# Output gates and z as seven quarter products in a stage of their own; the first SSD convs between the mLSTM heads; merge gates beside and behind the SSD groups

## The chip, the core and the metric

The program runs on one core of a Trainium2 chip. The metric is the device time of one execution in microseconds, the median of several runs. One execution was also taken by the hardware profiler; all rows here come from it. The engines are called as the profile calls them: PE (TensorE, matmuls), PEld (its weight loads), DVE (VectorE), ACT (ScalarE), POOL (GpSimd) and SP (SyncE, which issues the DMAs).

## What is computed

One layer of a hybrid decoder over 1072 rows: 16 meta tokens, 8 x 4 sample tokens, 1024 prompt tokens. All operands are float32.

```
u  = x @ w_in        # columns: mLSTM q/k, v, o, i, f; Mamba z, x/B/C, dt; merge gates
ya = W_a( sigmoid(o) * headnorm(mLSTM(silu(conv4(q, k)), v, i, f)) )        # 4 heads
yb = W_b( groupRMS( SSD(silu(conv4(x, B, C)), dt) * silu(z) ) )             # 4 groups of 8 heads
x  = LN1(alpha * x + W_out( sig(g_a) * ya + sig(g_b) * yb ))
x  = LN2(alpha * x + W_down( silu(conv3(up)_a) * conv3(up)_b ))             # up = x @ w_up, 2 x 2816
```

The mLSTM and the SSD are recurrences over nine chunks (one of 48 rows, eight of 128).

## The kernel before

**Matmuls.** Features lie on partitions and tokens on columns. Each float32 operand is split in two (`split`, line 150: a rounded copy on ACT, the rest by a subtraction on DVE), and three matmuls make one product (`mm3`, line 166). A unit is one block of 128 output columns of `w_in`: eight blocks of the inner dimension, three pieces of some 354 tokens, three matmuls, so 72 (`gemm`, line 171). `wload` (line 155) brings a unit's weights ahead of time into the pool `wp`, two buffers for each of its three tags. Results go to PSUM, in a pool `gps` of three banks and a pool `rps` of five.

**Order.** The instructions are traced in the order of the program text and placed in each engine's queue by a planner, by priority and estimated times; each engine and SP's DMA queue then run their queue in order. Pools of tiles on one side of SBUF follow each other: the pools `p0`, `wvp` and `gp` of the first stage, `mp` of the mLSTM heads, `sp` of the SSD groups, `pa` of the projections. Between a pool and the next stand waits.

**Stages.** (1) Input norm, v tiles, gate rows (lines 229 to 450). (2) The mLSTM heads, lines 518 to 663: for each head two convs for q and k (`qk_units`), two units for the output gate o (`o_units`, line 533: a tanh into an SBUF tile), the chunk chain (`mlstm`) and the normalisation, multiplied by the gate (`mlstm_out`). (3) The SSD, lines 666 to 910: six convs stand ahead of group 0; then `weave` puts pieces of other work between the steps of a group: the z units of the group before (`z_steps`, line 839, product with tanh straight from PSUM), the six convs of the next group (`conv_steps`, line 480: one unit, then three passes of 1096 columns on DVE and two on ACT) and merge gates (`gate_steps`, line 470; 16 units, counts in `GATES`, line 45). In each chunk `begin` (line 703) loads decays for the group (`dec`, two buffers), masks them on POOL, takes exponentials on ACT; `end` (line 790) makes the chunk's output and state, and adds D times x by four instructions (line 823). The z units of group 3 and `z_norm(3)` stand behind the groups. (4) Projections: h tiles are loaded and split (`pair`, line 923) into the pool `pa`, multiplied by W_a, then y by W_b, then W_out and the norm. (5) The FFN. Its up projection makes 20 of 22 pairs of blocks by seven products of quarters instead of eight (Winograd's form of Strassen's scheme): `PRODUCTS`, `prepare` and the loop from line 1235; x and weights are added and subtracted by quarters beforehand (lines 1162 to 1166 for x), and partial sums are put together behind the products. Forms of weights are made five products ahead (`AHEAD`). Two pairs are made by plain units (`plain`, `act_steps`), then (6) the down projection and the last norm.

## Time and profile before

| | |
|---|---|
| median of 3 runs | 2450.86 us (2449.71 to 2451.61) |
| the profiled execution, its own time | 2447.88 us |
| its span, first to last instruction | 2445.8 us |
| mean granted clock of TensorE | 0.988 of full speed |
| PE busy | 2360.0 us (96%), 15315 matmuls |
| DVE busy | 1580.7 us (65%) |
| ACT busy | 874.3 us (36%) |
| POOL busy | 577.4 us (24%) |
| DMA | 273.58 MB, mean 112 GB/s |

A row of a timeline gives the start in us from the first instruction, the duration, the engine, the line of the kernel, the operation with output<-inputs, and in brackets the idle time of that engine before it and what ended it. A busy PE counts matmuls that overlap in its pipeline, so the spacing of matmuls is read from their count in a stretch.

### The profile page before, as it was taken

How to read it: one execution, taken by the hardware profiler on the slowest of the kernel's cores; microseconds unless marked ns; L12 is line 12 of the kernel's file. 1: busy time of each engine (PE TensorE's matmuls, PEld its weight loads, DVE VectorE, ACT ScalarE, POOL GpSimd, SP SyncE). 2: the span in 40 equal slices, each digit the busy share in tenths (PEclk: the TensorE clock that was granted, in tenths of full speed). 3: DMA queues.
4: the chain of work that ended last, by engine and by line, in shares of the span. 5: the costliest groups of instructions: out<-in, count | busy, mean ns of one | idle time of the engine just before them, and what ended most of it. 6: DMA issues, size and time to landing. Idle time of an engine off the chain costs nothing. (4 is left out here: it accounts for less than half of the span.)

```text
span 2445.8 us, 38900 instructions
## 1 busy us (share of the span) xinstructions
PE 2360.0 (96%) x15315; PEld 2244.2 (92%) x15315; DVE 1580.7 (65%) x2673; ACT 874.3 (36%) x1703; POOL 577.4 (24%) x611
## 2 busy tenths in 40 slices
PE   7999999999999999999979999998999999999996
PEld 5889988989989989989978999998999999999996
DVE  7656667567457757755446456477988888874338
ACT  6243333434234434433222112245544444431111
POOL 0010000233123223222100000044655655410004
PEclk9999999999999999999989999999999999999998
DMA  9233331333443353344345433244222222272121
GB/s 245 71 104 118 108 108 70 93 116 104 113 159 91 84 165 86 84 144 120 95 151 177 127 112 124 90 158 153 84 85 74 80 81 81 91 265 81 46 65 72
DMA packets 166343, 273.58 MB, mean 112 GB/s; under 512 B 38328, under 2 KB 109848, under 8 KB 166160
## 3 DMA queue, kind: packets, MB, share of 16 engines
q1 hardware_dynamic: 166160, 271.10, 35.9%
q8 instruction: 120, 1.97, 0.3%
q14 instruction: 63, 0.52, 0.1%
HBM read 204.76 MB, written 66.29 MB: 111 GB/s over the span
## 5 line engine op out<-in xcount | busy, mean ns | idle before, releaser
L167 PE MATMUL gps<-xh,whi 128*128 128x352 f32 (+4 forms) x1752 | 589.0, 336 | 0.0
L168 PE MATMUL gps<-xl,whi 128*128 128x352 f32 (+4 forms) x1752 | 571.1, 326 | 0.0
L169 PE MATMUL gps<-xh,wlo 128*128 128x352 f32 (+4 forms) x1752 | 570.9, 326 | 0.0
L167 PEld LDWEIGHTS gps<-xh,whi 128*128 128x128 f32 (+1 forms) x1752 | 329.4, 188 | 16.4 <-issue 12.2
L152 ACT ACTIVATE whi<-wst 128x1024 fp32r<-128x1024 f32 (+1 forms) x161 | 164.6, 1023 | 501.6 <-PE gps L168 305.0
L168 PEld LDWEIGHTS gps<-xl,whi 128*128 128x128 f32 (+1 forms) x1752 | 329.7, 188 | 12.5 <-issue 11.8
L169 PEld LDWEIGHTS gps<-xh,wlo 128*128 128x128 f32 (+1 forms) x1752 | 328.9, 188 | 1.0 <-issue 0.8
L153 DVE TENSOR_TENSOR wlo<-wst,whi 128x1024 fp32r<-128x1024 f32 (+1 forms) x161 | 199.7, 1242 | 178.4 <-ACT whi L152 178.0
L167 PE MATMUL gps<-ph,whi 128*128 128x352 f32 (+1 forms) x472 | 152.9, 331 | 15.9 <-ACT ph L152 10.7
L168 PE MATMUL gps<-pl,whi 128*128 128x352 f32 (+1 forms) x472 | 154.5, 327 | 0.8 <-DVE pl L153 0.7
L719 ACT ACTIVATE dec<-dec,tk 128x128 f32<-128x128 f32 (+1 forms) x288 | 90.3, 384 | 180.2 <-POOL dec L716 165.4
L169 PE MATMUL gps<-ph,wlo 128*128 128x352 f32 (+1 forms) x472 | 153.7, 326 | 0.5 <-DVE wlo L153 0.3
L1254 PE MATMUL rps<-x1l,wf 128*128 128x266 f32 (+1 forms) x480 | 137.3, 286 | 0.0
L1253 PE MATMUL rps<-x1h,wf 128*128 128x266 f32 (+1 forms) x480 | 137.3, 286 | 0.0
L1255 PE MATMUL rps<-x1h,wf 128*128 128x266 f32 x480 | 136.7, 285 | 0.0
L1119 DVE SCALAR_TENSOR_TENSOR mix<-mix,c_fcw 128x1072 f32<-128x1072 f32 x80 | 115.9, 1448 | 6.9 <-ACT mix L1117 6.9
L167 PEld LDWEIGHTS gps<-ph,whi 128*128 128x128 f32 x472 | 88.9, 190 | 19.5 <-ACT ph L152 16.0
L506 DVE SCALAR_TENSOR_TENSOR cv<-u,c_scw,cv 128x1096 f32<-128x1096 f32 x72 | 97.7, 1357 | 8.7 <-ACT cv L504 7.4
L167 PE MATMUL gps<-ah,whi 128*128 128x352 f32 x312 | 101.1, 325 | 0.0
L169 PE MATMUL gps<-ah,wlo 128*128 128x352 f32 x312 | 100.9, 323 | 0.0
L168 PE MATMUL gps<-al,whi 128*128 128x352 f32 x312 | 100.6, 323 | 0.0
L168 PE MATMUL rps<-pl,whi 128*128 128x352 f32 (+1 forms) x296 | 96.5, 326 | 0.0
(411 smaller groups left out, 5744.2 us busy)
## 6 DMA issues: line engine op xcount, KB each, us to landing
wst<-in_win SPq DMA_DIRECT2D x72, 512.0 KB, 3.8
raw<-in_wup SPq DMA_DIRECT2D x40, 512.0 KB, 3.4
dec<-btd SPq DMA_DIRECT2D x32, 512.0 KB, 5.5
gt<-gd SPq DMA_DIRECT2D x24, 529.0 KB
wst<-in_wout SPq DMA_DIRECT2D x24, 512.0 KB, 3.3
fd<-mix SPq DMA_DIRECT2D x22, 528.0 KB, 3.1
raw<-fd SPq DMA_DIRECT2D x22, 528.0 KB, 3.6
wst<-in_wdn SPq DMA_DIRECT2D x24, 384.0 KB, 3.7
```

The source lines that it names most:

```text
L152: S.activation(hi, src, AF.Copy)
L153: V.tensor_tensor(lo, src, hi.bitcast(F32), ALU.subtract)
L167: PE.matmul(out, ah, bh, start=start, stop=False)
L168: PE.matmul(out, ah, bl, start=False, stop=False)
L169: PE.matmul(out, al, bh, start=False, stop=stop)
L506: V.scalar_tensor_tensor(cv, u[:, j:j + 1096], cw[:, j:j + 1], cv, op0=ALU.mult, op1=ALU.add)
L719: S.activation(dec[:n, i, 0:n], dec[:n, i, 0:n], AF.Exp, bias=tk2[:n, c, g * 8 + i:g * 8 + i + 1], scale=1.0)
L1119: V.scalar_tensor_tensor(cv, u[:, j:j + 1072], fcw[:, m, j:j + 1], cv, op0=ALU.mult, op1=ALU.add)
L1253: PE.matmul(ps, wh_, a, start=new and k == 0, stop=False, **chk)
L1254: PE.matmul(ps, wh_, b, start=False, stop=False, **chk)
L1255: PE.matmul(ps, wl_, a, start=False, stop=k == 3, **chk)
```

## The change

- The output gates o (8 units) and z (16 units) get a stage of their own between the v tiles and the mLSTM heads, in a pool `tp`. The normed x is loaded again from DRAM by blocks, its four quarter forms are made and split (`make_forms`), and 12 pairs of units are made by seven products of quarters each (`seven`, the loop of the FFN's up projection made into a function, which that projection now calls too). tanh, and for z the product, is taken on the summed quarters; the results are written to DRAM (`od`, `zd`).
- Two merge gate units (`GATES[0]`) stand in the program behind the making of the x forms and ahead of the products.
- In the heads, `mlstm_out` loads the gates from `od`. The six convs of SSD group 0 are made between the heads (`FILLS`: two, one, one, two) and go through DRAM (`xsd`) to the SSD stage.
- `z_steps` reads z from `zd` in three pieces for each tile and multiplies; it is advanced step by step beside the next group's convs or gates. D times x is made in place on ACT, and DVE adds.
- The merge gates: two beside each of groups 0 to 2, four beside group 3, four behind the groups. Their pool of evacuation tiles `ev` moves to the other side of SBUF and lasts until the h tiles are made.
- In the up projection the two plain pairs' `act_steps` come ahead of the last four splits of x.

The core of the diff:

```
-GATES = (0, 6, 2, 2, 6)
+GATES = (2, 0, 2, 2, 2, 4, 4)
+FILLS = (2, 1, 1, 2)
...
+    def make_forms(src, dst):
+        b11, b12, b21, b22 = src
+        G.tensor_tensor(b11, b12, b11, ALU.subtract)
+        G.tensor_tensor(b12, b22, b12, ALU.subtract)
+        V.tensor_tensor(b22, b22, b11, ALU.subtract)
+        V.tensor_tensor(b21, b22, b21, ALU.subtract)
+        for t, d in zip((b11, b22, b12, b21), dst):
+            if d is not None:
+                split(*d, t)
...
+    def seven(pairs, raws, sums, X, tmp, xforms, evac, begin=None, between=None):
...
+        names = ("a11", "s1", "s2", "s4", "a12", "s3", "a22")
+        loads, forms, banks = {}, {}, {}
+        wf = [wp.tile([128, 2, 4, 128], F32R, tag=t, name="wf") for t in ("wl", "ws", "wh") for _ in range(2)]
+        sw = {nm: sums[q // 2][:, 512 * (q % 2):512 * (q % 2) + 512].rearrange("p (k c) -> p k c", c=128)
+              for q, nm in enumerate(("s1", "s2", "s4", "s3"))}
...
+        def prepare(n):
...
+            if n == 0:
+                load(0)
+            if p == 5 and i + 1 < len(pairs):
+                load(i + 1)
+            w = quarters(loads[i], ("a11", "a12", "a21", "a22"))
+            nm = names[p]
+            if nm == "s1":
+                G.tensor_tensor(sw[nm], w["a21"], w["a22"], ALU.add)
+            elif nm == "s2":
+                G.tensor_tensor(sw[nm], sw["s1"], w["a11"], ALU.subtract)
+            elif nm == "s4":
+                G.tensor_tensor(sw[nm], w["a12"], sw["s2"], ALU.subtract)
+            elif nm == "s3":
+                G.tensor_tensor(sw[nm], w["a11"], w["a21"], ALU.subtract)
+            forms[n] = wf[n % 6][:, 0], wf[n % 6][:, 1]
+            split(*forms[n], sw[nm] if nm in sw else w[nm])
...
+        for n in range(AHEAD):
+            prepare(n)
+        for i in range(len(pairs)):
...
+            for p, xf in enumerate(xforms):
+                n = 7 * i + p
+                prepare(n + AHEAD)
+                wh, wl = forms.pop(n)
+                bank = "acxcaxd"[p]
+                new = p < 3 or p == 6
+                chk = {} if new else dict(skip_group_check=True)
+                for j, (t0, w_) in enumerate(HP):
+                    if new:
+                        banks[bank, j] = (rps if bank in "ac" or (bank, j) == ("x", 0) else gps)()
+                    ps = banks[bank, j][:, 0:w_]
+                    for k in range(4):
+                        h, l = xf(k)
+                        a, b = h[:, t0:t0 + w_], l[:, t0:t0 + w_]
+                        PE.matmul(ps, wh[:, k], a, start=new and k == 0, stop=False, **chk)
+                        PE.matmul(ps, wh[:, k], b, start=False, stop=False, **chk)
+                        PE.matmul(ps, wl[:, k], a, start=False, stop=k == 3, **chk)
+                    s1, s5 = X[:, j, 0:w_], X[:, 2 + j, 0:w_]
+                    if p == 0:
+                        S.copy(s1, ps)
+                    elif p == 1:
+                        S.copy(s5, ps)
+                    elif p == 2:
+                        u2 = banks["u2", j] = tmp()[:, 0:w_]
+                        V.tensor_tensor(u2, ps, s1, ALU.add)
+                    elif p == 3:
+                        evac(i, "12", t0, w_, ps, banks["u2", j])
+                    elif p == 4:
+                        evac(i, "11", t0, w_, ps, None)
+                    elif p == 5:
+                        V.tensor_tensor(s1, ps, s1, ALU.add)
+                        evac(i, "22", t0, w_, s1, s5)
+                    else:
+                        evac(i, "21", t0, w_, ps, s1)
+                if between:
+                    between(i, p)
...
+        raws = [tp.tile([128, 2 * HC], F32, name=f"raw{q}") for q in range(4)]
+        sums = [tp.tile([128, 1024], F32, name=f"sum{q}") for q in range(2)]
+        X = tp.tile([128, 4 * 266], F32, name="X")
+        tq = [[tp.tile([128, 4, HC], F32R, name=f"t{f}{p}") for p in "hl"] for f in range(4)]
+        for q in range(4):
+            G.memset(raws[q][:, TC:], 0.0)
...
+            b = raws[2 * (k % 2):2 * (k % 2) + 2]
+            dma(b[0][:, 0:TC], xd[k])
+            dma(b[1][:, 0:TC], xd[4 + k])
+            make_forms([t[:, h * HC:(h + 1) * HC] for t in b for h in range(2)],
+                       [[t[:, k] for t in tq[f]] for f in range(4)])
+        for _ in range(GATES[0]):
+            run(gate_steps(next(gates)))
+        def etile(n):
+            return tp.tile([128, 266], F32, tag="e", name="e", bufs=5)[:, 0:n]
+        jobs = [(M_O + q, od, q) for q in range(8)] + [(M_Z + q, zd, q) for q in range(16)]
+        jobs += [(M_GT + q, gd, q) for q in list(gates)[:16 - sum(GATES)]]
+        gates = iter(range(GATES[0] + 16 - sum(GATES), 16))
+        def evac(i, quarter, t0, n, a, b):
+            m, to, q = jobs[2 * i + (quarter[0] == "2")]
+            c = a
+            if quarter != "11":
+                c = etile(n)
+                if quarter == "12":
+                    V.tensor_tensor(c, a, b, ALU.add)
+                elif quarter == "21":
+                    V.tensor_tensor(c, b, a, ALU.subtract)
+                else:
+                    G.tensor_tensor(c, a, b, ALU.add)
+            if to is zd or quarter == "11":
+                e = etile(n)
+            else:
+                e = c
+            S.activation(e, c, AF.Tanh, scale=0.5)
+            if to is zd:
+                V.scalar_tensor_tensor(e, e, 1.0, c, op0=ALU.add, op1=ALU.mult)
+            t0 += HC * (quarter[1] == "2")
+            n = min(n, TC - t0)
+            dma(to[q, :, t0:t0 + n], e[:, 0:n])
+        def xq(k0, h):
+            def f(k):
+                return [t[:, k0 + k, CUT + h * HC:CUT + (h + 1) * HC] for t in (xh, xl)]
+            return f
+        def tf_(f):
+            return lambda k: [t[:, k] for t in tq[f]]
+        seven([(I["win"][jobs[q][0]], I["win"][jobs[q + 1][0]]) for q in range(0, len(jobs), 2)], raws, sums, X,
+              lambda: tp.tile([128, 266], F32, tag="u2", name="u2", bufs=2),
+              [xq(0, 0), tf_(0), tf_(1), xq(4, 1), xq(4, 0), tf_(2), tf_(3)], evac)
...
+        def fill_unit(q):
             out = []
-            for j in range(2):
-                w = win_load(M_O + 2 * h + j)
-                to = mtile([128, TC], "to", 2)
-                def evac(_, t0, n, ps, to=to):
-                    S.activation(to[:, t0:t0 + n], ps, AF.Tanh, scale=0.5)
-                gemm(w, NTC, xc_rhs, evac)
...
-        def mlstm_out(h, hs, mvs, to):
+        def mlstm_out(h, hs, mvs):
+            to = []
+            for j in range(2):
+                to.append(mtile([128, TC], "to", 2))
+                dma(to[j], od[2 * h + j])
...
         qk = qk_units(0)
-        to = o_units(0)
+        fills = iter(range(6))
         for h in range(4):
             st = mlstm(h, *qk)
-            if h:
-                to = o_units(h)
+            for _ in range(FILLS[h]):
+                fill_unit(next(fills))
             if h < 3:
                 qk = qk_units(h + 1)
-            mlstm_out(h, *st, to)
-        for _ in range(GATES[0]):
+            mlstm_out(h, *st)
+        for _ in range(GATES[1]):
             run(gate_steps(next(gates)))
...
                     V.tensor_tensor(tmp, tmp, iv, ALU.add)
+                for i in range(4):
+                    S.activation(xs[i][:, t0:t0 + n], xs[i][:, t0:t0 + n], AF.Copy,
+                                 scale=Dc[:, 4 * g + i:4 * g + i + 1])
...
                 for i in range(4):
-                    V.scalar_tensor_tensor(xs[i][:, t0:t0 + n], xs[i][:, t0:t0 + n], Dc[:, 4 * g + i:4 * g + i + 1],
-                                           tmp[:, i, 0:n], op0=ALU.mult, op1=ALU.add)
+                    V.tensor_tensor(xs[i][:, t0:t0 + n], xs[i][:, t0:t0 + n], tmp[:, i, 0:n], ALU.add)
                 if c == 8:
...
         def z_steps(g, xs):
             sqa = None
             for i in range(4):
-                w = win_load(M_Z + 4 * g + i)
                 y = xs[i][:, CUT:T]
-                def evac(j, t0, n, ps, y=y):
+                for t0, n in NTC:
                     tt = evt(n)
-                    S.activation(tt, ps, AF.Tanh, scale=0.5)
-                    V.scalar_tensor_tensor(tt, tt, 1.0, ps, op0=ALU.add, op1=ALU.mult)
+                    dma(tt, zd[4 * g + i, :, t0:t0 + n])
                     V.tensor_tensor(y[:, t0:t0 + n], y[:, t0:t0 + n], tt, ALU.mult)
-                for j, _ in enumerate(gemm_steps(w, NTC, xc_rhs, evac)):
-                    if j < 2:
...
-            if g:
-                yield from z_steps(g - 1, xs)
-            for i in range(4):
-                if g < 3:
-                    for j, _ in enumerate(xs_steps(g + 1, i, nxt)):
-                        if j == 1 and g and i == 0:
-                            z_norm(g - 1)
-                        yield
-            if g < 3:
-                yield from bc_steps(g + 1, nbc)
+            zs = z_steps(g - 1, xs) if g else iter(())
+            done = not g
+            for q in range(6 if g < 3 else 0):
+                for j, _ in enumerate(xs_steps(g + 1, q, nxt) if q < 4 else bc_steps(g + 1, q - 4, nbc)):
+                    if q < 2 and j:
+                        next(zs, None)
+                    if q == 3 and not done:
+                        run(zs)
+                        z_norm(g - 1)
+                        done = True
+                    yield
             for k in range(n_gates):
                 for j, _ in enumerate(gate_steps(next(gates))):
-                    if j == 1 and g == 3 and k == 0:
+                    next(zs, None)
+                    if j == 1 and k == 1 and not done:
+                        run(zs)
                         z_norm(g - 1)
+                        done = True
                     yield

         xs, bc, old = [], [], None
-        for i in range(4):
-            run(xs_steps(0, i, xs))
-        run(bc_steps(0, bc))
+        for q in range(6):
+            t = stile([128, T], "xs", 8) if q < 4 else stile([128, T], "bc", 4)
+            dma(t, xsd[q])
+            (xs if q < 4 else bc).append(t)
         for g in range(4):
             nxt, nbc = [], []
-            units = 4 * (g > 0) + 6 * (g < 3) + GATES[1 + g]
-            weave(ssd(g, xs, bc), work(g, old, nxt, nbc, GATES[1 + g]), 3 * units)
+            units = 6 * (g < 3) + GATES[2 + g]
+            weave(ssd(g, xs, bc), work(g, old, nxt, nbc, GATES[2 + g]), 3 * units)
             old, xs, bc = xs, nxt, nbc
         run(z_steps(3, old))
         z_norm(3)


...
-    evg = tc.tile_pool(name="evg", bufs=3)
-    evp = evg.__enter__()
     for m in gates:
         run(gate_steps(m))
...
+        make_forms([mix_[q][:, h * HC:(h + 1) * HC] for q in (k, 4 + k) for h in range(2)],
+                   [[t[:, k % 2] for t in tf[f][k // 2]] for f in range(3)] + [None])
+    for i in range(PLAIN):
+        run(act_steps(i, *raws[2 * i:2 * i + 2]))
     for k in range(4):
         split(x1p[k][0][:, HC:2 * HC], x1p[k][1][:, HC:2 * HC], mix_[4 + k][:, 0:HC])
```

## Rows read from the trace of the kernel before

**Rows 1.** Busy us of each engine by stretch, granted clock, DMA share, GB/s

```profile
core 0: us, PE busy (x) PEld busy (x) DVE busy (x) ACT busy (x) POOL busy (x), PEclk, DMA share, GB/s
145.60:425.30 279.70, 279.62 (x1636) 254.88 (x1635) 177.61 (x484) 101.28 (x229) 21.56 (x45) 1.00 0.32 106
425.30:496.10 70.80, 70.80 (x436) 70.74 (x435) 36.52 (x41) 29.42 (x66) 13.67 (x26) 1.00 0.33 92
862.80:1046.60 183.80, 180.80 (x1196) 167.90 (x1196) 125.36 (x185) 73.07 (x174) 53.42 (x57) 1.00 0.40 113
1046.60:1200.60 154.00, 151.62 (x1014) 138.85 (x1012) 80.83 (x141) 50.23 (x125) 36.02 (x32) 0.99 0.44 127
1200.60:1255.40 54.80, 54.80 (x338) 54.45 (x336) 24.54 (x38) 12.77 (x20) 0.00 (x0) 1.00 0.23 80
1260.80:1281.20 20.40, 10.12 (x39) 9.52 (x40) 6.62 (x20) 2.18 (x2) 0.32 (x8) 0.50 0.56 210
1275.20:1303.60 28.40, 24.18 (x120) 21.84 (x121) 17.02 (x14) 8.50 (x8) 0.00 (x0) 0.89 0.85 313
1750.00:2150.00 400.00, 400.00 (x3251) 400.00 (x3250) 331.06 (x462) 190.34 (x348) 232.56 (x228) 1.00 0.27 87
```

**Rows 2.** Timeline of PE behind the last z unit: start, us, what, idle, releaser

```profile
1261.29 3.78 PE L869 MATMUL rps<-ones,u 128*34 128x1 f32 x18 [5.71 <-DVE u L857]
1267.58 0.38 PE L875 MATMUL rps<-ident,rsd 128*9 128x128 f32 x1 [2.51 <-DVE rsd L147]
1275.24 0.66 PE L167 MATMUL gps<-ph,whi 128*128 128x354 f32 x1 [7.28 <-ACT ph L152]
```

**Rows 3.** Timelines of PE and of POOL behind the second half's v tiles

```profile
145.59 0.33 PE L167 MATMUL gps<-xh,whi 128*128 128x358 f32 x1
...
148.81 0.46 POOL L524 MEMSET qmask<- 128x432 f32 x1 [146.37 <-DMA vd<-vt]
```

**Rows 4.** Timelines of SP and ACT at the first h loads

```profile
1270.01 0.34 SPq L925 DMA_DIRECT2D pf<-hd  x1
...
1274.11 1.08 ACT L152 ACTIVATE ph<-pf 128x1058 fp32r<-128x1058 f32 x1 [14.17 <-DMA pf<-hd]
1277.85 1.09 ACT L152 ACTIVATE ph<-pf 128x1058 fp32r<-128x1058 f32 x1 [2.66 <-DMA pf<-hd]
```

**Rows 5.** Quarter forms of the up stage: POOL's timeline, then instructions by tile

```profile
1700.33 1.42 POOL L1162 TENSOR_TENSOR mix<-mix 128x530 f32<-128x530 f32 x1
...
L1164 DVE TENSOR_TENSOR mix<-mix x4: 693/696/698, 1709.9 to 1719.6; 128x530 f32<-128x530 f32 x4
L153 DVE TENSOR_TENSOR tf<-mix,tf x12: 693/695/1848, 1706.5 to 1722.7; 128x530 fp32r<-128x530 f32 x12
L152 ACT ACTIVATE tf<-mix x12: 629/640/671, 1703.4 to 1721.0; 128x530 fp32r<-128x530 f32 x12
```

**Rows 6.** Timeline of PE at the first products of the up stage

```profile
1740.58 0.39 PE L1253 MATMUL rps<-tf,wf 128*128 128x266 f32 x1 [2.49 <-ACT wf L152]
...
1743.18 0.59 PE L1255 MATMUL rps<-tf,wf 128*128 128x266 f32 x1 [2.09 <-DVE wf L153]
```

**Rows 7.** Groups by line on DVE: busy us, mean ns, idle before

```profile
L153 DVE TENSOR_TENSOR wlo<-wst,whi 128x1024 fp32r<-128x1024 f32 (+1 forms) x161 | 199.7, 1242 | 178.4 <-ACT whi L152 178.0
...
L506 DVE SCALAR_TENSOR_TENSOR cv<-u,c_scw,cv 128x1096 f32<-128x1096 f32 x72 | 97.7, 1357 | 8.7 <-ACT cv L504 7.4
...
L823 DVE SCALAR_TENSOR_TENSOR xs<-xs,c_Dc,tmp 128x128 f32<-128x128 f32 (+1 forms) x144 | 60.5, 477 | 0.5
```

**Rows 8.** Timelines in SSD group 3 around one chunk: SP, POOL, DVE

```profile
1134.67 0.37 SPq L707 DMA_DIRECT2D dec<-btd  x1
...
1150.09 0.37 SPq L707 DMA_DIRECT2D dec<-btd  x1
...
1141.30 1.09 POOL L716 TENSOR_SCALAR_AFFINE_SELECT dec<-dec 128x1024 f32<-128x1024 f32 x1 [2.33 <-DMA dec<-btd]
...
1145.31 1.22 DVE L738 TENSOR_TENSOR dec<-dec,rps 128x1024 f32<-128x1024 f32 x1 [3.69 <-ACT dec L719]
```

More of the change, by code (lines that the diff above doesn't have):

```diff
@@ L215 @@
     xp = xp_cm.__enter__()
-    xh = xp.tile([128, KD, T], F32R, name="xh")
-    xl = xp.tile([128, KD, T], F32R, name="xl")
+    xh = xp.tile([128, KD, CUT + 2 * HC], F32R, name="xh")
+    xl = xp.tile([128, KD, CUT + 2 * HC], F32R, name="xl")
+    zero = rc.tile([128, KD, 2], F32, name="zero")
+    V.memset(zero, 0.0)
+    split(xh[:, :, T:], xl[:, :, T:], zero)
     def x_rhs(k, t0, n):
@@ L518 @@
+    with ExitStack() as c1:
         mp = c1.enter_context(tc.tile_pool(name="mp", bufs=1))
@@ L678, in xs_steps, with bc_steps, alloc @@
             yield from conv_steps(sp, M_XS + m, scw[:, m], I["scs"][m], O["sco"][m], alloc)
-        def bc_steps(g, out):
-            for m in (16 + g, 20 + g):
-                def alloc():
-                    out.append(stile([128, T], "bc", 4))
-                    return out[-1]
-                yield from conv_steps(sp, M_XS + m, scw[:, m], I["scs"][m], O["sco"][m], alloc)
+        def bc_steps(g, q, out):
+            m = 16 + 4 * q + g
+            def alloc():
+                out.append(stile([128, T], "bc", 4))
+                return out[-1]
+            yield from conv_steps(sp, M_XS + m, scw[:, m], I["scs"][m], O["sco"][m], alloc)
         def weave(rec, work, n):
@@ new lines, in up_evac @@
+    def up_evac(i, quarter, t0, n, a, b):
+        if quarter == "11":
+            put_copy(uA, t0, n, a)
+        elif quarter == "12":
+            V.tensor_tensor(uA[:, 16 + HC + t0:16 + HC + t0 + n], a, b, ALU.add)
+        elif quarter == "22":
+            G.tensor_tensor(uB[:, 16 + HC + t0:16 + HC + t0 + n], a, b, ALU.add)
+        else:
+            put(lambda to, x, y, f: V.tensor_tensor(
+                to, f(b[:, x:y]) if f else b[:, x:y], f(a[:, x:y]) if f else a[:, x:y], ALU.subtract), uB, t0, n)
@@ new lines, in up_between @@
+    def up_between(i, p):
+        nonlocal end
+        i += PLAIN
+        if p == 2:
+            run(end)
+            u_begin(i, uA)
+            u_begin(22 + i, uB)
+            end = act_steps(i, uA, uB)
+        if p < 2 or p > 3:
+            next(end, None)
+        if i == 21 and p > 1 and p - 2 < FPARTS[0]:
+            first.append(act_load(p - 2))
+    seven([(I["wup"][i], I["wup"][22 + i]) for i in range(PLAIN, 22)], raws, (sw1, sw2), X, tmp_tile,
+          [half(0, 0), form(0), form(1), half(4, 1), half(4, 0), form(2), half(0, 1)],
+          up_evac, between=up_between)
```

136 lines of the change are left out of this document (28 added, 108 removed).

## The prediction

> **What bounds the kernel now.** I read the table by stretch first [rows 1]. TensorE (PE) is busy all of the mLSTM stretch (279.6 of 279.7 us) and of the last z units (54.8 of 54.8), and misses 3.0 of 183.8 us in SSD group 2. So PE's work sets the time in nearly every stage, and a product that is saved there is time that is saved. Only one long hole is left: the PE timeline behind the last z unit [rows 2] waits 5.71, 2.51 and 7.28 us, and the granted clock stands at 0.50 from 1260.8 to 1281.2 us (1.2 instead of 2.4 GHz) [rows 1].
>
> **Products.** A unit is 8 blocks x 3 time pieces x 3 matmuls = 72. The z stretch holds 338 matmuls in 54.80 us, 162 ns each, so 24 units (8 of o, 16 of z) are 1728 x 0.162 = 280 us. The changed stage makes 12 pairs x 7 products x 2 pieces x 4 blocks x 3 = 2016 matmuls of 264 to 266 columns. The existing stage of this shape runs 3251 in 400.00 us, 123 ns each: 248 us. Saved: 32 us; with the 160 ns of the shorter pieces it would be 29. I take **-31**. The new stage should hold that spacing: the existing one does it with VectorE (DVE) busy 331 and GpSimd (POOL) 233 of 400 us, and it carries the FFN's conv besides, which the new one exchanges for one tanh and, for z, one more DVE pass for each quarter. Its 8 output writes for each pair lie in SP's queue ahead of the next weight loads, but the forms are made five products (15 us) ahead.
>
> The Trainium skill (TensorE: Matmul & The Clock Gate, "Back-to-back issue gap") speaks against shorter matmuls: it says that in a stream of weight load and matmul the spacing was about 81 ns at 128 columns and 131 ns at 512, so it hardly shrinks with the columns. An estimate between those figures gives about 99 ns at 265 and 110 at 352: 2016 x 99 = 200 against 1728 x 110 = 190 us, a loss of 10 us instead of the gain. The rows differ (123 and 162 ns, nearly proportional to the columns), and I go by the rows.
>
> **The start of the new stage.** All of a pool's tiles wait until the pool before it is gone: the matmuls of the v tiles end at 145.59 us, and the first memset of the next pool waits for the last v write until 148.81 [rows 3]. Today convs need no tile of that pool at first, so PE goes on. In the changed kernel the x quarters can't be loaded before that, and what covers them is two gate units, 2 x 11.7 = 23.3 us, of which 3.2 pass before the pool opens. The chain, for four blocks of which two share the buffers: first load 4.1 us (issue 1270.01 to use 1274.11 [rows 4]); POOL subtracts two halves, 2 x 1.4 us, DVE two, 2 x 0.7, then four splits of 0.7 on DVE with 0.64 on ScalarE (ACT) beside them [rows 5]. Block 0 is done 4.1 + 2.8 + 1.4 + 2.8 = 11 us after the pool opens. Block 2 takes its buffers: load to 15, POOL to 18, DVE to 22. The first weights go into the same buffers: load to 26, split to 27. So PE would start the products 30 us behind the v tiles, with 23 covered: 7 us idle, and some 3 us at half clock, as behind the stop ahead of the existing stage, which waited 2.49 and 2.09 us for its first forms [rows 6]. **+10**, between +4 (the loads overlap better) and +20 (POOL and DVE slow each other: one split of the twelve took 1.85 us).
>
> **The end of the new stage.** Its pool closes with the last z write, about 4 us behind the last matmul; the q conv meanwhile fills three PSUM banks (11.7 us), as today behind the v tiles, and its weights need buffers that the last products hold. **+1** (0 to +4).
>
> **mLSTM heads.** 8 o units leave (already counted), 6 convs come in from the front of the SSD stage, where they stood alone: 70.80 us, with PE busy all of it [rows 1]. Moved PE work costs nothing in itself. DVE matters: those six convs stand beside 36.5 us of DVE, 6.1 each (three passes of 1.36 us and a split of 1.24 [rows 7] among it), an o unit only a split. The stretch becomes 279.7 - 23 = 256 us long with 177.6 - 10 + 37 = 204 us of DVE, 80% instead of 64%. The heads' chain goes through DVE in every chunk and a 1.36 us pass can stand in front of it; what that costs is not in this trace, so: **+3**, 0 to +15, nearer the low end since SSD groups run with DVE at 68% and lose under 2%.
>
> **From heads to SSD.** Today six convs cover the change of pools and the first group's loads. After, the last conv's passes (three of 1.36 us and, by my estimate, as much again on ACT and DVE) and its write of 548 KB (4 us, as the load of [rows 4]) end some 13 us behind its matmuls, and only then can the pool open and six tiles come in (3.3 MB; 313 GB/s was moved in the busiest stretch [rows 1], so 10 to 13 us). Convs of the next group are there to fill it, but their results need the pool's tiles after three PSUM banks (11.7 us). **+5**, 0 to +15.
>
> **SSD groups 0 to 2.** Four units fewer each: about 184 - 47 = 137 us. VectorE has 125.4 us now in group 2; without z's splits and products 114, and the D product of 144 instructions at 477 ns [rows 7] is split between ACT and a plain add, which I set at no less than half. That is 80% of 137 at most. z's values now arrive by 48 reads, on three tiles that the gates also use, in the queue of SP (SyncE) ahead of the decay loads. **+3**, -4 to +15. The chunk chain does not bind yet: a decay tile is requested at 1134.67 us, lands for POOL at 1141.30, is multiplied on DVE from 1145.31 for 1.2 us and frees its buffer for the next request at 1150.09 [rows 8]. From request to ready are 11.9 us, 13.4 with the matmuls that free it; two buffers allow a chunk every 6.7 us, and 137 us give one about every 11.
>
> **Group 3 and its tail.** Group 3 keeps 4 of 10 units: 154 - 70 = 84 us, about 7.1 a chunk against the 6.7: the chain is next in line. Its DMA ran at 0.44 of 154 us, 68 us; with six weight loads and six writes of gates less and the z reads more, about 60 in 84. Behind it come twelve z reads on three tiles (four rounds of some 4 us, 16) and the sums and the root (from 1261.29 to the pool's opening at 1270.01, 9 [rows 2, 4]), 26 in all, before the pool opens for the h tiles (first use 5 us later, then one about every 4 us [rows 4]). Today all of that stands open: 15.5 us of stops [rows 2], 5 lost to half clock (10.1 us busy in the 20.4 [rows 1]), and 28.4 - 24.2 = 4 in the slow start, 25 in all. Four gate units behind the group (46.7 us) are longer than 26 + 5, so I take **-21**, with 4 for what remains (-25 to -5), and **+10** (0 to +30) for group 3 and for the z reads behind it, since PE takes its instructions in a fixed order and may stand before the sums.
>
> **The up stage.** Two FFN conv units move ahead of four x splits on DVE; the stop of 2.09 us for a weight split may go: **-2** (-5 to +2).
>
> **Sum.** -31 + 10 + 1 + 3 + 5 + 3 - 21 + 10 - 2 = -22. The profiled execution took 2447.88 us, of which 2445.8 are span, so 2426 of that kind; it is 3 us under the median of the runs (2450.86), and the same difference from the median gives **2429 us**. The ends of the terms added up are about -60 and +70, but they won't all fall on one side.
>
> **Rivals.**
> Slower, the decay chain takes over: if the round trip under denser traffic grows to what passes today from one request to the next (15.4 us [rows 8]) plus the 6.9 behind its landing, a chunk costs 11.2 us. That costs group 3 nine times 4 us, 37, and groups 0 to 2, at about 11 themselves, some 5 each: +52 in place of the +13 of these terms, 2468 us. It decides from a landing of about 7.3 us on in group 3 (6.6 now) and 15 in the others. For it: group 3 has 0.4 us of room. Against it: in the others there is much room. 0.12.
> The setup stays open: SP, POOL and DVE in a row, and the heads held by DVE, both at their upper ends (+10, +12): 2451, no change. 0.12.
> The tail's hole stays: gates are drawn forward into group 3, or stand behind the sums in PE's order; without the 21 us it is 2450, no change. For it: PE's order is fixed ahead from estimated times. Against: the work itself suffices. 0.07.
> Spacing follows the instructions, not the columns (what the skill's figures point to): 2016 x 162 = 327 instead of 248 us, 2508. The rows of the existing stage speak against it: 0.01.
> Better: costs behind cover (setup +4, none in the heads, between the pools and in group 3): 2429 - 6 - 3 - 5 - 10 = 2405. 0.18.
> The diff can't do less than it says in products: the gate counts add up to 16, so the paired jobs are just the 24 units.
>
> **How the numbers follow.** My forecast, within some 15 us, has 0.50; better 0.18; no change 0.19, of which half falls each side of the 0.2% (5 us) that a measurement here can tell from none; slower 0.13. Predicted is the likeliest, 2429. The range leaves out half of the better case below 2404 and most of the slower beyond 2464. Faster 0.75, same 0.11, slower 0.14.
>
> **What would show it.** The new stage: 84 x 24 matmuls at 123 ns, PE full, about 248 us. Before it one stop of 4 to 12 us with a clock of 0.50 behind it. The stops of [rows 2] gone or under 5 us in all, with gate matmuls in their place. Group 3 at 85 to 95 us, its waits on the decay tiles. In the heads and the groups DVE near 80% and PE's waits under 2%. I'm wrong if the new stage runs slower than 123 ns, if groups 0 to 2 stay over 150 us, or if PE stands over 15 us at any of the three new changes of pools.

## The result: slower, and the profile after

The changed kernel takes 2473.35 us (median of 4 runs, 2463.88 to 2476.02) against 2451.24 for the kernel before: 1.0083 of it, 95% interval 1.0055 to 1.0111. I had predicted 2429. Measured once more beside other kernels (run e17_same, below) it came to 2466.13 us, 1.0073 (1.0057 to 1.0089). So it is some 18 to 20 us slower, not 22 faster. The profiled execution of after took 2476.02 us, 28 more than that of before (2447.88); the forecast was 22 less, so 50 us are to be found. It is the slowest of ten executions of this program (2460.62 to 2476.02), and that of e17 took 2464.44: about 12 of the 50 us come and go from one execution to the next.

The stages of after in one table: the new product stage, the heads, the four SSD groups (each from its first transposes), and what stands behind them. Columns as in [rows 1].

```profile
core 0: us, PE busy (x) PEld busy (x) DVE busy (x) ACT busy (x) POOL busy (x), PEclk, DMA share, GB/s
176.60:424.00 247.40, 246.89 (x1977) 246.16 (x1978) 132.03 (x239) 100.43 (x226) 84.87 (x70) 0.99 0.31 100
424.00:702.00 278.00, 276.11 (x1603) 249.84 (x1603) 210.26 (x533) 114.60 (x250) 35.32 (x71) 0.99 0.45 144
702.00:842.50 140.50, 130.49 (x840) 114.69 (x838) 96.59 (x139) 72.68 (x206) 50.00 (x60) 0.96 0.53 149
842.50:993.70 151.20, 141.83 (x917) 127.18 (x916) 113.15 (x169) 74.56 (x196) 51.03 (x57) 0.95 0.50 138
993.70:1138.60 144.90, 138.10 (x918) 124.63 (x917) 115.38 (x169) 73.44 (x192) 49.56 (x55) 0.99 0.50 144
1138.60:1242.00 103.40, 90.31 (x597) 74.70 (x595) 71.19 (x123) 48.98 (x138) 36.94 (x33) 0.93 0.60 170
1242.00:1304.00 62.00, 52.94 (x293) 51.95 (x292) 25.52 (x47) 15.98 (x22) 0.00 (x0) 0.86 0.51 163
```

The product stage starts when it was forecast to (176 us). Its row holds 1977 of the 2016 matmuls; the last one starts at 428.7 us, so the stage takes 252 us, 248 and some 4 that the half clock at its start costs. By the forecast's terms group 3 would have ended at 1200 us (176 + 3 for that half clock + 248 + 1 + 264 for heads and pool change + 3 x 137 + 3 for groups 0 to 2 + 84 + 10); it ends at 1242. So 42 of the 50 us are lost by the end of the groups. PE is full in the product stage and has holes in each group, with granted clocks of 0.93 to 0.99; in groups 2 and 3 of before it missed 3.0 and 2.4 us at a clock of 1.00 and 0.99 [rows 1].

Each group has two phases: the sample rows (from the last chunk product of one group to the first of the next) and the chunks. First four phases of before (chunks and samples of groups 0 and 1), then the same of after:

```profile
541.60:667.20 125.60, 125.60 (x852) 118.27 (x851) 77.36 (x103) 49.01 (x122) 33.66 (x33) 1.00 0.39 109
667.20:722.20 55.00, 54.01 (x339) 48.84 (x338) 27.73 (x45) 16.45 (x37) 13.11 (x11) 1.00 0.54 165
722.20:850.70 128.50, 128.28 (x871) 120.47 (x870) 94.51 (x139) 56.05 (x134) 39.72 (x46) 1.00 0.35 90
850.70:907.40 56.70, 53.93 (x337) 48.83 (x336) 29.03 (x46) 17.51 (x41) 13.19 (x11) 1.00 0.51 163
```

```profile
744.20:830.30 86.10, 81.88 (x557) 73.00 (x556) 70.71 (x101) 47.32 (x131) 31.03 (x37) 0.96 0.47 123
830.30:883.10 52.80, 46.54 (x267) 40.08 (x266) 31.90 (x50) 20.18 (x55) 14.67 (x17) 0.90 0.62 192
883.10:981.60 98.50, 95.39 (x653) 87.18 (x652) 81.26 (x121) 54.11 (x140) 36.38 (x41) 0.98 0.43 109
981.60:1031.10 49.50, 44.43 (x265) 38.96 (x264) 31.43 (x49) 20.01 (x55) 15.14 (x17) 0.97 0.64 203
1031.10:1126.50 95.40, 93.67 (x653) 85.65 (x653) 83.96 (x122) 54.16 (x140) 34.58 (x40) 1.00 0.43 113
1126.50:1169.90 43.40, 37.48 (x219) 31.16 (x218) 19.10 (x35) 15.22 (x42) 11.73 (x11) 0.92 0.56 173
1169.90:1239.50 69.60, 62.42 (x436) 52.83 (x434) 55.23 (x98) 35.56 (x104) 26.16 (x23) 0.95 0.62 167
```

Between samples of groups 0 and 1 PE had 339 matmuls before, 267 after, yet the phase went only from 55.0 to 52.8 us: one unit of 72 was taken away and 2.2 us came back. The clock columns give the second half of the loss: 0.90 over 52.8 us means 10.6 us at the half level, and over the seven rows it is 38 us at half, some 19 us lost if PE was busy all that time. The waits of PE in these phases, of after and then of before (in all, times, longest):

```profile
PE rps L894 <- ACT acol L301: 11.1, 3, 4.2
PE rps L930 <- DMA s<-in_s0T: 5.9, 4, 2.7
PE rps L968 <- DVE dec L908: 4.6, 2, 3.2
PE rps L1036 <- DVE u L1024: 2.5, 1, 2.5
PE gps L173 <- ACT u L600: 2.4, 2, 1.2
PE rps L907 <- DVE tmp L979: 1.7, 2, 1.2
```

```profile
PE rps L724 <- ACT acol L197: 4.8, 3, 2.5
PE rps L760 <- DMA s<-in_s0T: 1.1, 3, 0.5
PE rps L875 <- DVE rsd L147: 0.4, 2, 0.2
```

With the smaller rows PE stood 34 us in after and 6 in before: 28 us more of stops, and some 17 more in clock. These 45 us aren't the 42 one for one: the forecast had set aside 13 for the groups (+3 and +10), and in the first samples of group 0 (702 to 744 us) PE stood 5.8 us where it had stood 1.9.

The longest kind, on `acol`, is at the change of groups. It starts at a decay load on SP (834.23), which lands for POOL 6.7 us later, goes through the exponentials on ACT, and only behind these (and a weight split and an evacuation) in ACT's queue stands the copy for which PE waits. The timelines of SP, POOL, ACT and PE:

```profile
834.23 0.39 SPq L877 DMA_DIRECT2D dec<-btd  x1
...
840.92 1.09 POOL L886 TENSOR_SCALAR_AFFINE_SELECT dec<-dec 128x1024 f32<-128x1024 f32 x1 [9.93 <-DMA dec<-btd]
...
842.05 1.57 ACT L889 ACTIVATE dec<-dec,tk 128x128 f32<-128x128 f32 x5 [8.26 <-POOL dec L886]
...
843.87 0.97 ACT L889 ACTIVATE dec<-dec,tk 128x128 f32<-128x128 f32 x3
844.74 1.04 ACT L158 ACTIVATE whi<-wst 128x1024 fp32r<-128x1024 f32 x1
845.69 0.45 ACT L583 ACTIVATE evt<-gps 128x352 f32<-128x352 f32 x1
846.03 0.21 ACT L300 COPY acol<-xs 128x32 f32<-128x32 f32 x1
...
846.40 0.41 PE L894 MATMUL rps<-ident,acol 128*48 128x128 f32 x1 [3.61 <-ACT acol L301]
```

From the request to the end of the stop are 12.2 us, and PE had other work for 8.6 of them. The row on `dec` (L968) is the same chain without the detour. Behind the groups the hole of [rows 2] is smaller, not gone; PE's timeline there:

```profile
1264.44 0.66 PE L173 MATMUL gps<-xh,whi 128*128 128x354 f32 x1 [6.34 <-ACT evt L583]
1272.32 3.78 PE L1036 MATMUL rps<-ones,u 128*34 128x1 f32 x18 [2.72 <-DVE u L1024]
```

The first stop is of a new kind: a trailing gate has no evacuation tile, because twelve reads of z hold the three.

### The profile page after: what moved, and what is told of

Its sections match the earlier page's. It is cut to its first block, busy times and chain, and to the rows that moved or that the text cites. A ratio compares the mean times of both kernels' runs of the same rounds, so it can differ in the third digit from the quotient of the medians.

```text
span 2474.1 us, 40641 instructions
## 1 busy us (share of the span) xinstructions
PE 2356.4 (95%) x15603; PEld 2233.5 (90%) x15603; DVE 1675.8 (68%) x2871; ACT 972.8 (39%) x1996; POOL 662.9 (27%) x695
## 2 busy tenths in 40 slices
DMA packets 191122, 310.62 MB, mean 126 GB/s; under 512 B 41080, under 2 KB 131032, under 8 KB 190928
## 5 line engine op out<-in xcount | busy, mean ns | idle before, releaser
L173 PE MATMUL gps<-xh,whi 128*128 128x358 f32 (+5 forms) x1176 | 404.7, 344 | 12.6 <-ACT evt L583 6.3
L175 PE MATMUL gps<-xh,wlo 128*128 128x358 f32 (+5 forms) x1176 | 393.9, 335 | 0.0
L174 PE MATMUL gps<-xl,whi 128*128 128x358 f32 (+5 forms) x1176 | 391.5, 333 | 0.0
L173 PEld LDWEIGHTS gps<-xh,whi 128*128 128x128 f32 (+1 forms) x1176 | 226.6, 193 | 27.2 <-issue 9.7
L159 DVE TENSOR_TENSOR wlo<-wst,whi 128x1024 fp32r<-128x1024 f32 (+1 forms) x137 | 170.2, 1244 | 105.6 <-ACT whi L158 105.5
L174 PEld LDWEIGHTS gps<-xl,whi 128*128 128x128 f32 (+1 forms) x1176 | 226.3, 192 | 10.9 <-issue 10.3
L175 PEld LDWEIGHTS gps<-xh,wlo 128*128 128x128 f32 (+1 forms) x1176 | 226.7, 193 | 5.2 <-issue 4.7
L274 PE MATMUL rps<-x1h,wf 128*128 128x266 f32 (+1 forms) x480 | 137.8, 287 | 1.7 <-ACT mix L279 1.7
L276 PE MATMUL rps<-x1h,wf 128*128 128x266 f32 (+1 forms) x480 | 137.1, 286 | 0.0
L159 DVE TENSOR_TENSOR wf<-raw,wf 128x512 fp32r<-128x512 f32 x96 | 105.1, 1096 | 32.8 <-ACT wf L158 31.5
L613 DVE SCALAR_TENSOR_TENSOR cv<-u,c_scw,cv 128x1096 f32<-128x1096 f32 x72 | 103.1, 1432 | 17.1 <-ACT cv L611 16.7
L173 PE MATMUL rps<-ph,whi 128*128 128x352 f32 (+1 forms) x296 | 96.3, 325 | 0.0
```

What stands on the lines that cost most here:

```text
L159: V.tensor_tensor(lo, src, hi.bitcast(F32), ALU.subtract)
L173: PE.matmul(out, ah, bh, start=start, stop=False)
L174: PE.matmul(out, ah, bl, start=False, stop=False)
L175: PE.matmul(out, al, bh, start=False, stop=stop)
L274: PE.matmul(ps, wh[:, k], a, start=new and k == 0, stop=False, **chk)
L276: PE.matmul(ps, wl[:, k], a, start=False, stop=k == 3, **chk)
```

## Experiments

Times are compared by their ratio to the kernel before on the same chip; 0.01 of it is 24.5 us, and the changed kernel counts as 1.0073 (e17_same), the lower of its two measurements. Three theories at first: A, the reads of z hold up the groups; B, the decay chain does; C, too few units stand beside a group, so that any latency shows.

**No reads of z.**

```
-                    tt = evt(n)
-                    dma(tt, zd[4 * g + i, :, t0:t0 + n])
-                    V.tensor_tensor(y[:, t0:t0 + n], y[:, t0:t0 + n], tt, ALU.mult)
+                    V.tensor_tensor(y[:, t0:t0 + n], y[:, t0:t0 + n], xh[:, i, t0:t0 + n].bitcast(F32), ALU.mult)
```

> The changed kernel (2473 us) without the 48 reads of z: z_steps multiplies by a piece of the normed x that lies in SBUF, so the product and the sums stay and only the reads and their wait for the three evt tiles go; the output isn't that of the reference. Theory A (the reads hold up the groups: convs of the next group behind the freeing of xs, 6 us of PE stops on u L600; s0 loads behind reads in SP's queue, 8; sums, 5; gate evacuation behind the groups, 6; and the half clock behind each stop): 2428 to 2445 us. Theory B (the chunk's decay chain holds them up: acol 11, dec 6): 2465 to 2478. Theory C (too few units beside each group, so that one wait taken away is followed by the next): 2453 to 2465.

2460.23 us, 1.0035: 9 us gained. The stop on `evt` goes, but the stops on `acol` become 16.7 us. The time is in C's range, and A falls as the main cause. (Group 0 has no reads of z beside its chunks at all, the first being issued at 844 us, and its chunks miss 4.2 of 86.1 us.)

**No decay loads.**

```
+                if c == 0:
                     dma(dec[:n, :, 0:n], btd[...].partition_broadcast(n))
-                    G.affine_select(out=dec, in_=dec, ...
+                    G.affine_select(out=dec, in_=xl[:, 0, 0:1024]..., ...
```

The exponentials of these chunks take a small bias, so that the values stay finite.

> The changed kernel without the 32 decay loads of chunks 1 to 8 (512 KB each): GpSimd's select reads a tile that lies in SBUF and writes dec as before, so the two dec buffers, the select, the exponentials and the product stay; the output isn't that of the reference. Theory A (reads of z): 2462 to 2476, only lighter traffic. Theory B (decay chain; PE's stops on acol, which stands in ScalarE's queue behind exponentials that wait for the load, and on dec, 17 us in all, and the half clock behind them): 2435 to 2450. Theory C (cover): 2453 to 2465.

2437.32 us, 0.9943: 32 us gained, as B expected. No stop on `acol` is left, those on `dec` are 2.2 us:

```profile
PE rps L931 <- DMA s<-in_s0T: 4.1, 2, 2.4
PE rps L954 <- DVE xws L309: 3.4, 1, 3.4
PE gps L173 <- ACT u L600: 2.6, 2, 1.3
PE rps L904 <- DVE dec L909: 2.2, 3, 1.2
```

**Five acol tiles** (`bufs=3` to `bufs=5` in `a_cols`).

> The changed kernel with five acol tiles instead of three, so that all five of a group's first transposes can be fed before the exponentials of chunk 1 stand in ScalarE's queue. Theory B: the stops of 3.6, 3.3 and 4.2 us at the group changes go, with the half clock behind two of them: 2455 to 2464. Theory A: 2468 to 2476. Theory C: 2463 to 2470, since PE then stops a little later for s0 or the exponentials.

2463.83 us, 1.0045: 7 us, where the ranges of B and C meet. The stops on `acol` are gone; those on s0 rose from 7.9 to 11.7 us and on u from 6.2 to 7.6 (702 to 1243 us in both). That is C's picture.

**D times x on VectorE again** (the old `scalar_tensor_tensor` for ACT's copy and the add).

> The changed kernel with D times x back on VectorE as one instruction (scalar_tensor_tensor), ScalarE's 144 copies gone. If ScalarE's added work (1.3 us in each of 36 chunks) holds the exponentials and evacuations: 2455 to 2465. If it is covered: 2470 to 2482, as VectorE's four adds become longer by 0.2 to 0.6 us a chunk.

2461.49 us, 1.0041: 8 us. The intervals of e3 and e4 (1.0030 to 1.0060, 1.0027 to 1.0056) just touch that of the changed kernel, so these two gains are not shown.

**Decays laid out by chunk.** The same bytes, but one load reads 4 KB in a row for each partition, not eight rows of 512 B.

```
-    btd = dr.tile([32, T], F32, name="btd")
+    btd = dr.tile([8, 32, 128], F32, name="btd")
+    btd0 = dr.tile([32, NA], F32, name="btd0")
-        dma(btd, bs)
+        dma(btd0, bs[:, 0:NA])
+        dma(btd.rearrange("c p t -> p c t"), pc(bs))
-                dma(dec[:n, :, 0:n], btd[g * 8:(g + 1) * 8, t0:t0 + n].partition_broadcast(n))
+                dma(dec[:n, :, 0:n], (btd[c - 1] if c else btd0)[g * 8:(g + 1) * 8].partition_broadcast(n))
```

> The changed kernel with the decays of chunks 1 to 8 laid out by chunk in DRAM, so that a load of 512 KB reads 4 KB in a row for each partition instead of eight rows of 512 B; nothing else differs. In the profile such a load took 5.9 us (median) to land, other loads of 512 KB 3.4 to 4.4. Theory B1 (the decay chain binds by the time of its transfer): landing 4 us or less, 2450 to 2462. Theory B2 (it binds by its place in SP's queue and by two buffers; the transfer itself matters little): 2466 to 2475, whatever the landing.

2444.14 us, 0.9963 (0.9948 to 0.9978): 27 us gained, more than expected. From issue to landing a load takes, in after and then here (min, median, max):

```profile
DMA to landing us min/median/max: 5.0/5.9/7.1
```

```profile
DMA to landing us min/median/max: 3.3/4.2/4.9
```

1.7 us less in each of 32 loads empties the chunk phases; here the chunks of group 0, the samples behind them and the chunks of group 1:

```profile
744.20:823.60 79.40, 78.75 (x557) 70.77 (x557) 70.35 (x102) 47.33 (x132) 33.91 (x37) 1.00 0.45 136
823.60:873.50 49.90, 45.73 (x267) 39.56 (x266) 32.74 (x49) 20.38 (x55) 14.61 (x17) 0.93 0.63 201
873.50:966.90 93.40, 93.34 (x653) 85.57 (x652) 83.90 (x125) 54.42 (x142) 37.70 (x41) 1.00 0.40 119
```

86.1 and 98.5 us became 79.4 and 93.4 with the same matmuls, PE nearly full and the clock back at 1.00. The stops on `acol` fell from 11.1 to 2.5 us. Other loads of the chunks landed a little sooner too (E, of the same decays, 3.6 us instead of 4.8, pieces of z 3.1 instead of 3.7, medians); what part of the gain comes by them no run divides.

**The same two in the kernel before**, as controls.

> The kernel before with the decay loads of chunks 1 to 8 left out in the same way as in e2_nodec; the output isn't that of the reference. If the chain binds only once four units fewer stand beside each group: 2440 to 2451 (its PE stops on acol are 4.8 us there, on dec none). If it held the groups all along, 2415 to 2435, a gain like the 36 us of e2_nodec.

2443.32 us, 0.9961: 10 us, not 32.

> The kernel before with the decays laid out by chunk. Without any decay load it gained 8 us (e6_b_nodec), so if the chain binds only where units are few: 2444 to 2451, a quarter or less of what the same edit gave the changed kernel.

2445.31 us, 0.9977 (0.9966 to 0.9988): 6 us, not 27. So the chain costs little where the groups are thick with units and three times as much or more once units are gone.

**Eight units beside group 3** (`GATES = (2, 0, 2, 2, 2, 8, 0)`).

> The changed kernel with the four last gate units moved from behind the groups to beside group 3, so that eight units stand there instead of four. Group 3 takes 103 us now. If its stops are only a lack of cover: 105 to 125 us with eight units, and behind it the sums and h loads stand open again (some 15 to 20 us with the half clock): 2460 to 2475 in all. If units beside a group cost their full 11.7 us: 150 us, and 2485 to 2500 in all.

2488.52 us, 1.0150: 19 us slower than the changed kernel, the second case's time. The chunk phase is full, and behind it PE stands open:

```profile
1181.00:1264.20 83.20, 83.20 (x591) 75.97 (x590) 48.34 (x73) 37.72 (x115) 24.71 (x22) 1.00 0.50 126
1264.20:1304.00 39.80, 14.64 (x93) 13.56 (x92) 19.37 (x41) 6.68 (x8) 1.06 (x1) 0.69 0.47 156
...
1298.57 3.78 PE L1036 MATMUL rps<-ones,u 128*34 128x1 f32 x18 [23.51 <-DVE u L1024]
```

From the last chunk of group 2 to that of group 3 are 143 us (1121.1 to 1264.2) instead of 113: four units cost 30 us where 47 is their own time, between the two cases. The time of the second case comes from the tail, which lies open for longer than I expected.

**Plain units in the new stage**, instead of the seven products.

```
-        seven([(I["win"][jobs[q][0]], ...
+        for m, to, q in jobs:
+            gemm(win_load(m), NTC, xc_rhs, plain_evac)
```

> The changed kernel with the 24 units of its new stage made as plain units (72 matmuls of 352 to 354 columns each) instead of seven products; the stage, its quarter forms of x (made, not used), tanh, the writes and everything behind stay. If the products are worth what the two traces' spacing says (1728 x 162 against 2016 x 123 ns): 31 us slower than the changed kernel, 2500 to 2508, less up to 7 if no forms of weights need be waited for at its start. If the spacing gained is given back elsewhere: 2475 to 2490.

2485.51 us, 1.0150: 19 us slower. Its stage makes 1235 matmuls in 200 us, 162 ns each, against 1626 in 200 us, 123 ns, in the changed kernel:

```profile
200.00:400.00 200.00, 200.00 (x1235) 200.00 (x1234) 37.58 (x51) 39.83 (x68) 0.00 (x0) 1.00 0.28 93
```

```profile
200.00:400.00 200.00, 200.00 (x1626) 200.00 (x1625) 101.19 (x195) 82.96 (x187) 65.01 (x56) 1.00 0.31 100
```

The plain units need no forms, so the stop at the stage's start is spared with its half clock: 31 less 10 is 21. In the profiled executions the heads' first chunk product starts at 490.4 us here, at 464.3 in after and 462.3 in e17: 26 to 28 us for the stage with its start, so the gain of the products is there, and somewhat more than it. That the whole comes to less (12 and 24 us between these profiled executions, 19 by the ratios) lies in part with the groups behind, which ran 485.6 us here, 495.3 in after and 487.6 in e17 (see the order of the queues below).

**The kernel before with four gates behind its groups**, one part of the change alone.

```
-GATES = (0, 6, 2, 2, 6)
+GATES = (0, 6, 2, 2, 2)
-    ev = tc.tile_pool(name="ev", bufs=3)
+    ev = tc.tile_pool(name="ev", bufs=3, side="right")
```

(`ev` also stays open until the h tiles are made, as in the change.)

> The kernel before with one part of the change: four of the six gate units beside group 3 go behind the groups, with the evacuation tiles on the other side of SBUF. The gates then cover the sums, the root and the first h loads (25 us of stops, half clock and slow start in the rows of before). If group 3 gives back all of its four units (six stay): 2427 to 2436. If a group with six units is already short of cover: 2440 to 2448.

2429.76 us, 0.9923 (0.9900 to 0.9946): 19 us faster than before by the ratio, 21 by the medians. The stops of [rows 2] are gone. From the first chunk product to the last the groups ran 619.3 us instead of 656.5, so a group 3 with six units gave back 37 of the 47 us of its four.

**The same with 14 gates behind the groups** (`GATES = (0, 2, 0, 0, 0)`): units 8, 10, 10 and 4. (With no gate beside group 3, `z_norm(2)` is called there by a line of its own.)

> As e10_b_tail, with 14 gate units behind the groups: beside groups 0 to 3 stand 8, 10, 10 and 4 units instead of 12, 12, 12 and 10, with z straight from PSUM, no reads of z, D times x on VectorE. If lack of cover alone opens the stops (on acol, s0, dec, behind the decay loads), it loses 15 to 25 us against e10_b_tail, most of it in groups 0 and 3, and its group 0 shows idle PE and half clock as group 0 of the changed kernel does (4 us in the chunks, 6 between the groups). If the stops of the changed kernel come from what it adds beside the groups (reads of z, ScalarE's copies): within 5 us of e10_b_tail.

2442.29 us, 0.9964: 10 us worse than e10, between the two cases. The chunks of group 3, with z in PSUM and no reads, show what those of the changed kernel show:

```profile
997.20:1054.20 57.00, 51.73 (x381) 43.20 (x379) 48.66 (x83) 25.06 (x73) 24.67 (x23) 0.97 0.61 153
```

PE misses 5 of 57 us. So part of the loss comes by thin cover alone, without anything that the change adds there. Group 0 doesn't show it as expected (4 us in the chunks, 6 between the groups):

```profile
531.30:623.90 92.60, 91.47 (x636) 83.63 (x635) 76.68 (x103) 42.85 (x108) 33.83 (x37) 1.00 0.44 118
623.90:678.00 54.10, 51.64 (x315) 46.34 (x314) 27.50 (x47) 17.36 (x43) 12.64 (x11) 0.97 0.46 150
```

PE misses 1.1 and 2.5 us, against 4.2 and 6.3 in the changed kernel, whose phases hold fewer units (4.3 and 2.7, here 5.3 and 3.3).

**Both ways to mend it.** e12 has the layout, five acol tiles and D times x on VectorE; e7 also reads z of group 3 whole into free tiles, for which the last group's `xs` buffers are used:

```
+                if g == 3:
+                    zt = stile([128, T], "xs", 8)
+                    dma(zt[:, 0:TC], zd[4 * g + i])
```

> The changed kernel with four edits: decays by chunk in DRAM (e5_pack), five acol tiles (e3_acol5), D times x on VectorE (e4_dxdve), and the z of group 3 read into four free xs tiles, whole and early, instead of twelve pieces through the evt tiles (for the stops of 6.3 us on evt and 2.7 on the sums behind group 3). If the gains add up (10 + 12 + 15 + 10): 2425 to 2435, faster than both kernels. If each wait removed lets the next one show (theory C): 2440 to 2452.

> As e7_best2 (2427 us) without its fourth edit: z of group 3 again by twelve pieces through the evt tiles. If the stops on evt (6.3 us) and on the sums behind group 3 with the half clock behind them are what that edit took away: 2436 to 2444. If the three other edits made the gain: 2427 to 2431.

e12: 2439.00 us, 0.9958. e7: 2427.08 us, 0.9893 (0.9872 to 0.9913), faster than both kernels, as if the gains added up. The stop on `evt`, still 5.7 us in e12, is gone in e7; that edit is worth 12 us by the medians, 16 by the ratios.

> e7_best2 (2427 us) with two of the four gate units behind the groups moved beside group 3, which then has six. If a unit there costs about 7.5 us instead of 11.7 (e8_g8) and the tail still closes with two (23 us against some 10 for the products of z, 9 for the sums and the root, 5 to the first h tile): 2417 to 2423. If the tail opens: 2428 to 2440.

2436.06 us, 0.9943, the second case: with two gates moved to group 3 (`GATES = (2, 0, 2, 2, 2, 6, 2)`) the tail opens, PE waits 7.5 us for h tiles.

**What the order does by itself.** e9's groups ran 10 us shorter than those of the changed kernel (485.6 against 495.3 us from 1st to last chunk product), with the same code. But the groups of e17, the very same program, ran 487.6 us: so much differs between two executions of one order. Besides, each edit lets the planner order the queues anew. e13 moves one early conv to another head and changes nothing else; e14 adds the layout.

> The changed kernel with FILLS (1, 2, 1, 2) for (2, 1, 1, 2): one of the six early convs is made behind the second head instead of the first; no work is added or taken, and the code of the groups is the same. It measures what ordering the queues anew does by itself. If the small gains seen so far are of the edits: 2469 to 2477. If the order planned for the changed kernel was an unlucky one: 2460 to 2466, and the gains of 9 to 13 us can't be put down to their edits.

> e13 with the decays laid out by chunk (as e5_pack). If the shorter load is worth its 29 us whatever the order: 25 to 32 us faster than e13. If half of it was the order: 12 to 18 us faster than e13.

> The changed kernel itself, measured again. If its 2473 us stand (1.0083 of the kernel before): 2468 to 2476, and the gains of 9 to 13 us are more than chance. If the four runs were high: 2460 to 2467, and e1, e3, e4 and e13 are no gains that can be told from none.

e13: 2461.36 us, 1.0053 (1.0033 to 1.0073); e17, the changed kernel itself, 2466.13 us, each the second of its two cases. Their intervals overlap, so 5 us can be order or chance, and the 7 and 8 us of e3 and e4 stay unsettled. So do the 9 us of e1: its interval (1.0024 to 1.0045) stands clear of e17's, but not of e13's, and the order alone could have made them. e14: 2445.19 us, 0.9977, 19 us under e13 (16 by the medians), nearer its second case: the layout's gain stands, but as 16 to 27 us.

**Without the product stage.** The kernel before with e10's gates and the layout.

> The kernel before with four gate units behind the groups (e10_b_tail) and the decays laid out by chunk (e15_b_pack), no product stage. If the gains add up (21 and 6): 2421 to 2427, as fast as e7_best2 (2427), and the product stage is worth nothing net even there. If group 3's decay loads hide the gain of the layout: 2428 to 2432.

2422.51 us, 0.9886 (0.9872 to 0.9899): the two gains add up to 28 us, and the kernel without the stage is as fast as e7, which has it (0.9893).

## Point by point: why the prediction was wrong

**Right.** Products: 123 ns, PE full, 252 us with the half clock at the start; the traces put stage and start together at -26 to -28 against e9, where the terms said -21. Start: one stop of 7.13 us, from 169.6 to 176.8, and a clock of 0.50 from 172.4 to 182.7 us. Heads: by [rows 1] 1636 - 576 + 436 = 1496 matmuls were due, 1603 ran in the stretch of the table, of which 39 are still of the product stage and 68 more than due (by my count convs drawn forward, 11 us); from 428.9 us, and less these 11, it took 262 us, forecast 264 with the change of pools, with DVE at 76%.

**Up stage (-2): nothing.** The stops of [rows 6] became 1.73 and 0.75 us, but one of 2.28 us on a plain pair's weights is new, and from the first write of x1 to the last of the FFN's rows to `fd` both kernels take 474 us.

**Wrong, the step that failed: groups 0 to 2 (+3) and group 3 (+10).** Groups 0 to 2 were to take 414 us and took 437, with 11 us of their convs made before; group 3 was to take 94 and took 103. PE's waits there, forecast under 2%, were 5 to 13%. "The chunk chain does not bind yet" set an average against an average: a chunk every 6.7 us by the two buffers, one every 11 by the groups' length. But PE waited for the chain though the chunks of after came no faster than one every 8.7 us. My reading is that it binds by its length: from request to ready it takes 12 us [rows 8], and PE, whose order is fixed, must have that much other work at the place where it stands (8.6 of 12.2 us at the stop shown above). By the unit matmuls counted in each phase (72 to a unit), samples held 3.5 to 3.7 units in before and 2.0 to 2.7 in after, chunks 6.7 to 8.3 and 2.3 to 5.3. In after PE misses 1.7 and 3.1 us in the chunks with 5.3 units, 4.2 with 4.3, 7.2 with 2.3. As a whole even the thinnest phase has 23 us of units, more than the chain, so it is the place that counts; no run varied that alone. Nothing in the chain itself had to get worse: the landing went from 5.5 to 5.9 us in the median. The rival "the decay chain takes over" had the right mechanism and nearly the time (2468), and its condition was wrong: it was to decide from a landing of 7.3 us in group 3 and 15 in the others. e2, e5 and e14 show the chain, e6 and e15 that the missing units make it count. By e2 and e6 it accounts for some 32 - 10 = 22 of the 42 us, an estimate good to the 5 us or so that order and chance can make. I had put 0.12 on it.

**Wrong by size: the half clock.** I counted it behind the long stops alone. In the groups the short stops, 28 us more than before, went with another 17 us lost in clock.

**The tail (-21).** Right as a mechanism and as a size in the kernel before (e10: -19). In the changed kernel some 13 of the 21 came: from the end of group 3 to the first write of x1 are 481.5 us, 494.3 before, with four units behind the groups in both; that is the rest of the 50. (The sum of 16 and 9 in the prediction is 25, not 26; nothing hangs on it.) The gates share three tiles with twelve reads; these I had priced as a delay of the sums, not as a stop of the gates themselves. 6.34 + 2.72 us of stops with their half clock stayed, and reading z elsewhere gave 12 us (e12 to e7).

**Open.** What is left of the 42 us behind the chain may lie with cover (e11: 10 us, in another kernel), the reads (e1: 9, unsettled), ACT's copies (e4: 8, unsettled) and chance; these overlap, and no run here divides them.

## What to carry to other kernels

Units that fill the holes of a recurrence aren't free to take away, even where PE is 98% busy: count the cover at each place where PE must sit out a chain against the length of that chain, not the average pace over the group. Before moving such units, shorten the chain, here by the layout of one load; then try the cheap part alone: gates behind the groups and the layout gave 28 us without the product stage. And measure the same program again before reading gains of 10 us from one execution of each.

## What the hardware showed that was not expected

A load of 512 KB in rows of 512 B took 5.9 us to land, in rows of 4 KB 4.2 us (191122 DMA packets became 162722). The Trainium skill (DMA: Bandwidth & Descriptors, "Why small descriptors are slow (HBM only)") gives a fixed cost of about 3 cycles a packet beside 32 bytes a cycle; an estimate from that is 16% more for 512 B than for 4 KB, so 5.1 us where 4.2 was measured. The direction agrees, the gain here was twice as large.

Behind short stops the granted clock stood lower: the samples between groups 0 and 1, with stops of 3.6 and 2.7 us, ran at a mean of 0.90; the chunks of groups 0 and 1, at 0.96 and 0.98 in after, ran at 1.00 once the decays landed sooner (e5).
